# Second product of the FFN: part 7 after all chunks of parts 5, 6 and 3, on the bank of parts 1 and 6, with part 4 on that; the last norm regrouped; the first loads in small pieces

## The chip, the core and the metric

The kernel runs as one program on one core of a Trainium2 chip. The core has a matrix engine (TensorE; PE in the profile, PEld for its weight loads), three elementwise engines (VectorE or DVE, ScalarE or ACT, GpSimd or POOL), a synchronising engine (SyncE, SP), and 16 DMA engines. The metric is the device time of one execution in microseconds, the median of several runs. Before the change it was 1905.4 us (three runs, 1904.87 to 1906.9).

## What is computed

Two layers of a bidirectional encoder over 512 tokens of width 1024, everything in float32:

```python
for l in range(L):
    x = x + 0.5 * swiglu(rms_norm(x, ffn1_norm[l]), ffn1_w_in[l], ffn1_w_out[l])
    x = x + mixer(rms_norm(x, mix_norm[l]), mix_w_in[l], ...)
    x = x + 0.5 * swiglu(rms_norm(x, ffn2_norm[l]), ffn2_w_in[l], ffn2_w_out[l])
return rms_norm(x, final_norm)

def swiglu(x, w_in, w_out):
    g, u = jnp.split(x @ w_in, 2, axis=-1)
    return (jax.nn.silu(g) * u) @ w_out
```

So there are four feed-forward blocks (FFN), each with a first product (1024 to 2 x 2816) and a second (2816 to 1024). The change touches the second product of all four, the very beginning of the kernel, and the final norm.

## The kernel before

**Precision.** Each float32 operand is split into a high part (rounded to what TensorE reads as `fp32r`) and a low part (the rest). A product is three matmuls: high by high, low by high, high by low. For a weight tile the high part is made on ACT (line 181, or 176 with the sign changed) into `whi`, the low part on DVE (line 184 or 177) into `wlo`; there are three buffers of each. For an activation tile `split` and `hl` do the same (lines 298 and 299, or 301 and 302 with a gain).

**Weights.** A *granule* is 128 x 1024 numbers, 512 KB: two contraction tiles of 512 columns. `stage_items` lists all granules in the order of use. `Stream` issues their loads on SP's queue up to eight ahead into nine `raw` buffers; a second granule may be added to one by an accumulating DMA on POOL's queue (line 152) or by DVE (line 166).

**Strassen form.** The big products are done as seven block products, numbered 1 to 7, out of two-by-two blocks. In the second product of an FFN the contraction is cut in two halves, and each half into three chunks c = 0, 1, 2 of 3, 4 and 4 tiles (`CHUNK`), so each of the seven parts is done as three chunk products. One chunk product adds into a *pair* of PSUM banks, one for each block of 128 tokens. `steps` (line 667) is the order of chunk products: part 1 for all chunks, part 2 for all chunks, then 5, 6, 7, 3 for one chunk after the other, then part 4 for all chunks. `make(i)` prepares the activation operand of step i (a difference or sum on DVE in `comb`, line 659, then the split), and is called up to two steps ahead. For parts 1, 2 and 4 a granule is loaded as it is. Parts 5 and 7 load `d` and then add `c`, or `c` and then `a`, with the accumulating DMA; part 6 adds `a` to what part 5 left, and part 3 then adds `b`, both on DVE.

**Which bank holds what.** Parts 1 and 6 share one pair (`o1`): after part 1 has been subtracted from one quadrant of x, part 6 goes on adding into the same banks. Parts 7 and 4 share another pair (`o7`). Parts 2, 5 and 3 have one each. `update(ps, i, j, sign)` (line 662) adds or subtracts a pair to a quadrant of the residual x, on DVE, two instructions (line 665), one for each bank. In one FFN there are ten such updates, so 20 instructions.

**Order inside a chunk product.** `product` (line 458) takes granule by granule; `late_low` (line 449) issues, for a set of (bank, tile) pairs, the high and low activation matmuls with the high weights (lines 453, 454), and then those with the low weights (line 456). By default a granule serves both token blocks before the next granule comes. With `by_block` all granules serve token block 0 first and then block 1; before the change only the very last chunk product of the kernel uses it.

**Next stage.** `nxt.squares` sums the squares of a finished quadrant of x on ACT (line 335). `nxt.quad` transposes a finished quadrant for the next stage: eight PE transposes, then ACT and DVE work. In the three FFNs that are not the last one, quadrants (1,1) and (0,1) are transposed within part 4, chunk 0, inside a block where the order on DVE and ACT is the program's own.

**The start.** The gains (128 x 48) are loaded on ACT's queue (line 1506), and transposed x tiles and weight granules alternately on SP's (lines 1512 and 150): the first two x tiles (256 KB) on their own, then two by two; the first weight granule in two pieces. Nine matmuls on a tile of zeros (`warm`, line 138) run before anything has landed; ACT writes one column of `warm` by a Tanh (line 135), which also loads the table of that function. The first block is a plain product (`plain`, line 564): for each of eight contraction tiles, twelve matmuls into four banks named `cl`. `Norm.given` (line 342) scales an x tile by its gain, splits it, and keeps the scaled numbers in `raw` tiles named `xr` (line 350).

**The end.** In the last FFN, after part 4, x is normalised and written out. `gained` multiplies a half row block of x by the final gain on DVE (line 921); `scaled` multiplies a row block by its inverse root on ACT (line 926) and starts its transfer from SP's queue (line 927); `whole` does both at once on DVE (line 933). Row blocks 2 and 3 are finished early; for 0 and 1 the last quadrant of x comes from part 4, and `inverse` (line 391) works out one inverse root from the two sums of squares: a square root on ACT, then four small DVE instructions (lines 398 to 402). All of this is in an order written out by hand, and queued behind the last `wlo` of the kernel.

Of the kernel before, what the change touches and what calls it, by code (L numbers as in the profile page):

```python
# [29 lines left out]
WARM = 9  # L30
AHEAD = 2
# [61 lines left out]
def encoder_kernel(  # L93
    ctx: ExitStack, tc: tile.TileContext, xin, xtr, wst, gains, gfin, gbias, rpb, dft, chan, mask, ident_in, rot, out
# [40 lines left out]
    S.activation(warm[:, 0:1], ones, AF.Tanh)  # L135
# [5 lines left out]
    class Raw:  # L141
# [3 lines left out]
        def load(self, parts=1):  # L145
            if self.t is None:
                self.t = raw_pool[0](self.n)
                for c in range(0, self.n, self.n // parts):
                    cs = slice(c, c + self.n // parts)
                    nc.sync.dma_start(out=self.t[:, cs], in_=wst[GRAN_AT[self.key]][:, cs])  # L150
                if self.plus:
                    G.dma_start(out=self.t, in_=wst[GRAN_AT[self.plus]][:, 0 : self.n], accum_op=ALU.add)  # L152

    class Item:
        def __init__(self, raw, add=None, neg=False, stage=0, parts=1, pieces=1, then=None):
            self.raw, self.add, self.neg, self.stage, self.parts = raw, add, neg, stage, parts
            self.pieces, self.then = pieces, then

        def load(self):
            self.raw.load(self.pieces)  # L160
# [8 lines left out]
        def prep(self, nxt):  # L169
            n = self.raw.n  # L170
            hi = wp.tile([P, 1024], F32R, tag="whi", name=nm("whi"), bufs=3)[:, 0:n]
            lo = wp.tile([P, 1024], F32R, tag="wlo", name=nm("wlo"), bufs=3)[:, 0:n]
            t = self.raw.t
# [4 lines left out]
            else:  # L178
                for c in range(0, n, n // self.parts):
                    cs = slice(c, c + n // self.parts)  # L180
                    S.activation(hi[:, cs], t[:, cs], AF.Copy)  # L181
                    if nxt:
                        nxt.summed()
                    self.last = V.tensor_tensor(lo[:, cs], t[:, cs], hi[:, cs].bitcast(F32), ALU.subtract)  # L184
            if self.then:
                G.dma_start(out=t, in_=wst[GRAN_AT[self.then]][:, 0:n], accum_op=ALU.add)
            self.out = (hi, lo)

    def stage_items():
# [34 lines left out]
        def ffn(s):  # L224
            first = not items
            if first:
                for g in range(4):
                    add(Raw((s, "cl", g)), parts=2 if g < 2 else 1, pieces=2 if g == 0 else 1)
# [3 lines left out]
            for order in ((1,), (2,), (5, 6, 7, 3), (4,)):  # L232
# [85 lines left out]
    class Norm:  # L318
# [23 lines left out]
        def given(self, i, k, src):  # L342

            self.tiles(i)
            g = self.gain(4 * i + k)
            split(self.h[i][:, k, :], self.l[i][:, k, :], src, g)
# [37 lines left out]
        def terms(self, tb):  # L384

            e, f = small("e", 1), small("ef", 1)
# [1277 lines left out]
```

## Time and profile before

| what | value |
|---|---|
| median of three runs | 1905.4 us |
| the profiled execution's own time | 1904.67 us |
| its span, first to last instruction | 1902.9 us |
| PE busy | 1891.0 us (99% of the span), 9189 matmuls |
| DVE busy | 1606.4 us (84%) |
| ACT busy | 1161.2 us (61%) |
| transfers | 361.09 MB, on average 190 GB/s |
| granted TensorE clock, mean | 0.999 |

The span is the profile's; the execution's own time has 1.8 us more around it. The views read below are the profile page, the chain of work that ended last, the timeline (start, duration, engine, line, operation, tiles, and behind brackets the idle time before it with what ended it), the view of one tile's instructions (durations as least/median/most in ns), the table of stretches (busy time of each engine, then granted clock, DMA share and GB/s), and the DMA view. In the timeline a row such as `x2` stands for two instructions in a run; a PE duration includes the pipeline, so two matmuls follow each other more closely than their durations say.

### The profile page before, as it was taken

How to read it: one execution, taken by the hardware profiler on the slowest of the kernel's cores; microseconds unless marked ns; L12 is line 12 of the kernel's file. 1: busy time of each engine (PE TensorE's matmuls, PEld its weight loads, DVE VectorE, ACT ScalarE, POOL GpSimd, SP SyncE). 2: the span in 40 equal slices, each digit the busy share in tenths (PEclk: the TensorE clock that was granted, in tenths of full speed). 3: DMA queues.
4: the chain of work that ended last, by engine and by line, in shares of the span. 5: the costliest groups of instructions: out<-in, count | busy, mean ns of one | idle time of the engine just before them, and what ended most of it. 6: DMA issues, size and time to landing. Idle time of an engine off the chain costs nothing.

```text
span 1902.9 us, 25187 instructions
## 1 busy us (share of the span) xinstructions
PE 1891.0 (99%) x9189; PEld 1586.7 (83%) x9189; DVE 1606.4 (84%) x2000; ACT 1161.2 (61%) x1676; POOL 198.0 (10%) x246
## 2 busy tenths in 40 slices
PE   9999999999999999999999999999999999999998
PEld 7888888888888888888888888888888888888886
DVE  7877899586889987889997778995769899787899
ACT  6655665468566755566665556663675576555665
POOL 0101010310111010001010100103101101000010
PEclk9999999999999999999999999999999999999999
DMA  9777499322886776649877764974148867766594
GB/s 301 203 205 190 149 250 319 99 73 93 218 217 166 176 195 204 177 154 261 252 186 210 187 177 153 271 276 126 53 122 213 209 177 176 206 177 177 172 272 149
DMA packets 104924, 361.09 MB, mean 190 GB/s; under 512 B 12064, under 2 KB 14240, under 8 KB 104800
## 3 DMA queue, kind: packets, MB, share of 16 engines
q1 hardware_dynamic: 77856, 267.42, 40.1%
q0 software_dynamic: 26800, 92.04, 26.8%
q8 instruction: 72, 1.18, 0.2%
q14 instruction: 52, 0.43, 0.1%
q10 hardware_dynamic: 144, 0.02, 0.0%
HBM read 354.18 MB, written 2.11 MB: 187 GB/s over the span
## 4 chain that ended last, share of the span: by engine, by line
PE 99%; DVE 1%; ACT 0%; DVEq 0%; issue 0%; ACTq 0%
PE A L453 9%; PE A L454 9%; PE A L456 9%; PE o L453 7%; PE o L454 7%; PE o L456 7%; PE ps L292 5%; PE ps L293 5%; PE ps L294 5%; PE B L453 5%; PE B L454 5%; PE B L456 5%; PE C L454 2%; PE C L453 2%; PE C L456 2%; PE tr L546 2%
## 5 line engine op out<-in xcount | busy, mean ns | idle before, releaser
L181 ACT ACTIVATE whi<-raw 128x1024 fp32r<-128x1024 f32 (+1 forms) x528 | 546.4, 1037 | 418.9 <-PE A L454 124.6
L184 DVE TENSOR_TENSOR wlo<-raw,whi 128x1024 fp32r<-128x1024 f32 (+1 forms) x528 | 627.8, 1194 | 186.5 <-ACT whi L181 183.7
L152 POOL DMA_DIRECT2D raw<-in_wst_dram x158 | 136.2, 872 | 1282.0 <-DMA raw<-in_wst_dram 678.3
L166 DVE TENSOR_TENSOR raw<-raw,raw 128x1024 f32<-128x1024 f32 (+1 forms) x146 | 172.2, 1189 | 1.2
L454 PE MATMUL A<-whi,xl 128*128 128x512 f32 x384 | 149.5, 389 | 0.0
L453 PE MATMUL A<-whi,xh 128*128 128x512 f32 x384 | 149.4, 389 | 0.0
L456 PE MATMUL A<-wlo,xh 128*128 128x512 f32 x384 | 110.5, 389 | 0.0
L176 ACT ACTIVATE whi<-raw 128x1024 fp32r<-128x1024 f32 (+1 forms) x79 | 81.6, 1035 | 39.0 <-PE A L454 10.2
L177 DVE SCALAR_TENSOR_TENSOR wlo<-raw,whi 128x1024 fp32r<-128x1024 f32 (+1 forms) x79 | 92.9, 1190 | 11.6 <-ACT whi L176 11.6
L639 ACT ACTIVATE th<-sn,rh 128x512 f32<-128x512 f32 x80 | 56.9, 715 | 69.8 <-DVE sn L528 69.8
L523 ACT ACTIVATE sn<-A 128x512 f32<-128x512 f32 x96 | 56.4, 589 | 51.3 <-PE A L456 51.2
L456 PEld LDWEIGHTS A<-wlo,xh 128*128 128x128 f32 x384 | 72.1, 188 | 15.0
L454 PEld LDWEIGHTS A<-whi,xl 128*128 128x128 f32 x384 | 72.1, 188 | 14.8
L453 PEld LDWEIGHTS A<-whi,xh 128*128 128x128 f32 x384 | 72.1, 188 | 14.8
L453 PE MATMUL B<-whi,t1h 128*128 128x512 f32 x192 | 76.2, 397 | 0.0
L453 PE MATMUL A<-whi,t3h 128*128 128x512 f32 x192 | 75.3, 392 | 0.0
L453 PE MATMUL C<-whi,xh 128*128 128x512 f32 x192 | 74.9, 390 | 0.0
L453 PE MATMUL A<-whi,t2h 128*128 128x512 f32 x192 | 74.9, 390 | 0.0
L454 PE MATMUL B<-whi,t1l 128*128 128x512 f32 x192 | 74.8, 390 | 0.0
L454 PE MATMUL A<-whi,t3l 128*128 128x512 f32 x192 | 74.8, 390 | 0.0
L454 PE MATMUL C<-whi,xl 128*128 128x512 f32 x192 | 74.7, 389 | 0.0
L454 PE MATMUL A<-whi,t2l 128*128 128x512 f32 x192 | 74.7, 389 | 0.0
(410 smaller groups left out, 4785.7 us busy)
## 6 DMA issues: line engine op xcount, KB each, us to landing
raw<-in_wst_dram SPq DMA_DIRECT2D x466, 512.0 KB
raw<-in_wst_dram POOLq DMA_DIRECT2D x162, 512.0 KB, 7.7
raw<-in_wst_dram SPq DMA_DIRECT2D x30, 256.0 KB
vs<-v SPq DMA_DIRECT2D x12, 256.0 KB
bw<-in_rpb_dram SPq DMA_DIRECT2D x32, 68.0 KB
x<-in_xin_dram SPq DMA_DIRECT2D x4, 512.0 KB
raw<-in_wst_dram POOLq DMA_DIRECT2D x8, 256.0 KB, 8.1
dft<-in_dft_dram POOLq DMA_DIRECT2D x8, 256.0 KB, 6.0
```

The costliest lines, as they stand in the source:

```text
L152: G.dma_start(out=self.t, in_=wst[GRAN_AT[self.plus]][:, 0 : self.n], accum_op=ALU.add)
L166: V.tensor_tensor(self.raw.t, self.raw.t, self.add.t, ALU.add)
L176: S.activation(hi, t, AF.Copy, scale=-1.0)
L177: self.last = V.scalar_tensor_tensor(lo, t, -1.0, hi.bitcast(F32), ALU.mult, ALU.subtract)
L181: S.activation(hi[:, cs], t[:, cs], AF.Copy)
L184: self.last = V.tensor_tensor(lo[:, cs], t[:, cs], hi[:, cs].bitcast(F32), ALU.subtract)
L292: PE.matmul(ps, lh, rh, start=start, stop=False, skip_group_check=again)
L293: PE.matmul(ps, lh, rl, start=False, stop=False, skip_group_check=again)
L294: PE.matmul(ps, ll, rh, start=False, stop=stop, skip_group_check=again)
L453: PE.matmul(ps, lh, rh, start=start, stop=False, skip_group_check=again)
L454: PE.matmul(ps, ll, rh, start=False, stop=False, skip_group_check=again)
L456: PE.matmul(ps, lh, rl, start=False, stop=stop, skip_group_check=again)
```

## The change

It has three parts.

**1. The second product of each FFN.** The order of chunk products becomes: part 1, part 2, then 5, 6, 3 for one chunk after the other, then part 7 for all chunks, then part 4 for all chunks; the granules are listed in the same order. Part 7 now adds on into the pair of parts 1 and 6, and part 4 adds on into the same pair, so `o7` is gone; a quadrant that took two updates (one from each pair) takes one. The last chunk of part 7 and the first of part 4 are issued by token block. The transposes of quadrant (1,1) move from chunk 0 of part 4 to chunk 1.

**2. The end.** Row block 3 is finished before the last updates, one small term of row blocks 0 and 1 is made for both at once, row block 0 goes out in two halves, and row block 1 is multiplied by the final gain first; then ACT scales one half and sends it from ACT's own queue while DVE scales the other half, sent from SP's queue.

**3. The start.** The Tanh writes another tile than `warm`. The gains lie ahead of the transposed x in one array and come with the first x tile in one transfer; POOL copies them to their place. The first four x tiles and the first two granules come in pieces of 256 KB, x tile and weight piece in turn. The splits of the first four tiles are written out by hand, in a fixed order on DVE and ACT; the high part of the first two weight pieces is made on DVE instead of ACT. For the first two tiles the matmuls are ordered as all high by high, then all low by high, then all high by low.

```diff
-            for order in ((1,), (2,), (5, 6, 7, 3), (4,)):
+            for order in ((1,), (2,), (5, 6, 3), (7,), (4,)):
...
+            steps.append((3, c, lambda c=c: part(1, 1, c)))
+        for c in range(3):
             steps.append((7, c, lambda c=c: comb(part(0, 1, c), part(0, 1, c), part(1, 1, c), ALU.subtract)))
-            steps.append((3, c, lambda c=c: part(1, 1, c)))
...
-            key = {6: 1, 4: 7}.get(m, m)
+            key = {6: 1, 7: 1, 4: 1}.get(m, m)
...
-                ps[key], made.pop(i), list(range(len(CHUNK[0][c]))), c == 0 and m in (1, 2, 3, 5, 7), c == 2,
-                m in (4, 6), by_block=late and i == len(steps) - 1,
+                ps[key], made.pop(i), list(range(len(CHUNK[0][c]))), c == 0 and m in (1, 2, 3, 5), c == 2,
+                m in (4, 6, 7), by_block=(m, c) in ((7, 2), (4, 0)) or late and i == len(steps) - 1,
...
                     make(i + 2)
-                    nxt.quad(1, 1)
                     nxt.quad(0, 1)
             make(i + 2)
+            if m == 4 and c == 1 and not late:
+                nxt.quad(1, 1)
...
-            if m == 4 and c == 1:
-                update(ps[1], 1, 0, 1)
...
             elif m == 6:
-                update(ps[1], 1, 1, 1)
-            elif m == 7:
-                update(ps[7], 1, 1, 1)
-                nxt.squares(1, 1)
                 update(ps[1], 0, 1, -1)
...
+            elif m == 7:
+                update(ps[1], 1, 1, 1)
+                nxt.squares(1, 1)
...
+                    update(ps[1], 1, 0, 1, (0,))
+                    nxt.squares(1, 0, (0,))
+                    root = [nxt.inverse(b, e[:, b : b + 1], f[:, b : b + 1]) for b in range(2)]
+                    next(root[0])
+                    gained(0, 0)
+                    gained(0, 1)
+                    next(root[0])
+                    next(root[0])
+                    scaled(nxt, 0, 0)
+                    update(ps[1], 1, 0, 1, (1,))
+                    nxt.squares(1, 0, (1,))
+                    next(root[1])
+                    gained(1, 0)
+                    gained(1, 1)
+                    scaled(nxt, 0, 1)
+                    next(root[1])
+                    next(root[1])
+                    o_, _, _, to = half(1, 0)
+                    S.activation(o_, o_, AF.Copy, scale=nxt.inv[1])
+                    S.dma_start(out=to, in_=o_)
+                    o_, _, _, to = half(1, 1)
+                    V.tensor_scalar(o_, o_, nxt.inv[1], None, ALU.mult)
+                    nc.sync.dma_start(out=to, in_=o_)
...
-    S.activation(warm[:, 0:1], ones, AF.Tanh)
+    S.activation(sp.tile([P, 8], F32, tag="sq", name="tanh", bufs=2)[:, 0:1], ones, AF.Tanh)
...
-    S.dma_start(out=gn, in_=gains)
...
+        for kt in range(4):
...
+            ws.items[kt // 2].raw.piece(kt % 2 * T, (kt % 2 + 1) * T)
+        ws.fetch(2)
+        G.tensor_copy(gn, first_gains)
...
+                S.activation(xh, src[kt], AF.Copy, scale=g)
+                if kt == 0:
+                    norm.given_raw(0, 0, src[0], g)
+                if kt < 2:
+                    V.tensor_copy(wh[:, z], t)
+                else:
+                    S.activation(wh[:, z], t, AF.Copy)
+                V.scalar_tensor_tensor(xl, src[kt], g, xh.bitcast(F32), ALU.mult, ALU.subtract)
+                V.tensor_tensor(wl[:, z], t, wh[:, z].bitcast(F32), ALU.subtract)
+                if kt:
+                    norm.given_raw(0, kt, src[kt], g)
```

131 lines of the change are left out of this document (74 added, 57 removed).

## The prediction

> **What bounds the kernel.** I read the page first, then the chain of waits, then the timeline at both ends and at the seams of the second product.
>
> ```profile
> span 1902.9 us, 25187 instructions
> ...
> PE 1891.0 (99%) x9189; PEld 1586.7 (83%) x9189; DVE 1606.4 (84%) x2000; ACT 1161.2 (61%) x1676; POOL 198.0 (10%) x246
> ...
> PE 99%; DVE 1%; ACT 0%; DVEq 0%; issue 0%; ACTq 0%
> ```
>
> PE sets the time: 99% of the span and of the chain. What is not PE is 1902.9 - 1891.0 = 11.9 us, and nearly all of it lies before the first matmul and after the last. The change leaves the number of matmuls as it is, so it can gain at the two ends alone, and lose wherever PE, which has no gap now, gets one.
>
> **The start now.** From the chain of waits and the timeline:
>
> ```profile
> 2.73 4.02 PE ps L138 x9
> 6.75 0.43 PE cl L453
> ...
> 7.61 0.35 PE cl L453
> ...
> 8.20 0.23 PE cl L453
> ```
>
> ```profile
> 0.90 0.27 DVE L134 MEMSET warm<- 128x256 uint32 x1
> 1.18 1.28 ACT L135 ACT_TABLE_LOAD   x1 [1.18 <-PEq L1653]
> ...
> 2.73 4.02 PE L138 MATMUL ps<-warm 128*128 128x512 bf16 x9 [2.73 <-ACT warm L135]
> ...
> 4.51 0.72 ACT L301 ACTIVATE xh<-xt,gn 128x512 fp32r<-128x512 f32 x1 [1.84 <-DMA gn<-in_gains_dram]
> 4.51 0.62 DVE L350 TENSOR_SCALAR xr<-xt,gn 128x256 f32<-128x256 f32 x2 [3.35 <-DMA gn<-in_gains_dram]
> ...
> 5.14 1.25 ACT L181 ACTIVATE whi<-raw 128x512 fp32r<-128x512 f32 x2
> ...
> 5.27 0.75 DVE L302 SCALAR_TENSOR_TENSOR xl<-xt,gn,xh 128x512 fp32r<-128x512 f32 x1
> ...
> 6.19 0.99 PE L453 MATMUL cl<-whi,xh 128*128 128x512 f32 x1
> ...
> 7.09 0.72 ACT L301 ACTIVATE xh<-xt,gn 128x512 fp32r<-128x512 f32 x1 [0.71 <-DMA xt<-in_xtr_dram]
> ...
> 9.87 0.39 PE L453 MATMUL cl<-whi,xh 128*128 128x512 f32 x1
> ...
> 12.59 0.39 PE L453 MATMUL cl<-whi,xh 128*128 128x512 f32 x1
> ```
>
> The nine warm-up matmuls wait for ACT's table load, not for data, and end at 6.75, when the first operands (xh at 5.23, the first half of whi at about 5.8) are long there. A matmul then still takes 0.43; the step is 0.23 from about 8. So contraction tile 0 ends only at 9.87; tile 1 takes 12.59 - 9.87 = 2.72, the full-speed price of twelve.
>
> **The start after.** `warm` is free at 0.90 + 0.27 = 1.17, so the warm-up ends by 1.2 + 4.02 = 5.2. The gains were the last to land (4.51); they now come with x tile 0, so I leave the first operation at 4.5. ACT makes xh to 5.2; DVE makes two xr to 5.1, then the new copy of 512 numbers. No row shows it; bounds are half of the 0.62 (one row of 256, so 0.31) and the 0.75 of L302. I take 0.62, half of L181's 1.25, the same work: whi is there at 5.75. Tile 0 then ends at
>
> - 5.8 + 2.72 = 8.5 if the clock is full by then: gain 1.35;
> - if the clock comes 5.0 us after the first warm-up (2.73 to about 7.75 now), at 6.2: one slow matmul, gain 1.15;
> - if it comes at 7.75 whatever PE did: 4.5 matmuls at 0.43, 7.5 at 0.227, end 9.45, gain 0.4.
>
> I take **-1.0**, nearest the second, with something for the copy. Bounds: -0.4, and -1.95 if x tile 0 lands well before the gains did and only the warm-up's end (5.2 + 2.72 = 7.9) counts. Tile 1's xh is due at 8.5 and would be there at 7.09 + 0.72 = 7.8; its second weight piece now follows x tile 1, the same bytes into the queue as x tile 1 is now, so 7.1 and 7.7 after the copy: 0.8 of cover, and each tenth beyond it costs a tenth. POOL's copy of the gains, not seen in the trace, has from 4.5 to that xh.
>
> The Trainium skill (TensorE: Matmul & The Clock Gate, Part 1) says that the clock is released after about 3.4 us of sustained work counted in free-running windows. Here the trace shows 5.0 us from the first warm-up. By that rule the moment can be anywhere from 4.6 to 8 after the change, which spans the three cases above.
>
> **The second product, on PE.** The count of matmuls is the same. But a part that goes on in a bank that DVE has read starts with a slow matmul:
>
> ```profile
> L453 PE MATMUL o<-whi,c6h x88: 389/389/477, 264.0 to 1867.0; 128*128 128x512 f32 x88
> ...
> L453 PE MATMUL o<-whi,c7h x88: 389/389/390, 268.2 to 1872.5; 128*128 128x512 f32 x88
> ...
> L453 PE MATMUL o<-whi,c4h x88: 389/389/475, 319.8 to 1892.9; 128*128 128x512 f32 x88
> ```
>
> Parts 6 and 4 have a longest one of 477 and 475 ns against 389; part 7, which opens a fresh bank, has none. After the change part 7 goes on too, and part 4 waits once for each bank: two more of 0.087 in each of four FFNs, 0.7. Bounds 0 and +0.7; I take **+0.5**.
>
> The new wait is the seam of parts 7 and 4. Part 4 may not touch a bank before `update` has read part 7's sum. The block order gives cover: bank 0 is complete while PE still does block 1 of part 7's last chunk, 12 matmuls or 2.72; for bank 1 there is block 0 of part 4's first chunk, three tiles, 9 matmuls or 2.04. How fast does DVE answer?
>
> ```profile
> 1867.95 0.39 PE L453 MATMUL o<-whi,c7h 128*128 128x512 f32 x1
> ...
> 1868.24 1.21 DVE L184 TENSOR_TENSOR wlo<-raw,whi 128x1024 fp32r<-128x1024 f32 x1
> 1869.38 1.28 DVE L665 SCALAR_TENSOR_TENSOR x<-o,x 128x512 f32<-128x512 f32 x2
> ...
> 1878.83 0.39 PE L453 MATMUL o<-whi,c4h 128*128 128x512 f32 x1
> ...
> 1879.24 1.28 DVE L665 SCALAR_TENSOR_TENSOR x<-o,x 128x512 f32<-128x512 f32 x2
> ```
>
> Part 6 ends as part 7 begins, at 1867.95; its update starts 1.43 later, behind a `wlo`. Part 3 ends at 1878.83, answered after 0.41. With 0.68 for one update a bank is free 1.1 to 2.1 after it is complete: inside 2.72, and 0.1 past 2.04 at worst. Four seams: 0 to +0.4; I take **+0.2**. Queued behind the update on DVE are only later `wlo` and activation splits.
>
> **DVE and the transfers.** In parts 5, 6, 7, 3 both are full:
>
> ```profile
> 1819.00:1835.30 16.30, 16.30 (x73) 13.51 (x72) 16.30 (x18) 11.86 (x16) 2.74 (x4) 1.00 0.99 298
> ...
> 1862.50:1868.00 5.50, 5.50 (x26) 4.55 (x25) 5.50 (x8) 2.03 (x2) 0.00 (x0) 1.00 0.46 149
> ...
> L665 DVE SCALAR_TENSOR_TENSOR x<-o,x x80: 669/678/691, 244.1 to 1894.0; 128x512 f32<-128x512 f32 x80
> ```
>
> DVE is busy 16.30 of 16.30, the DMA share is 0.99 and falls to 0.46 only near the end. The change takes four of the 20 updates of each FFN away (80 rows in all), 4 x 0.6 = 2.4 us of DVE, off the path. Against that, parts 5, 6, 3 without part 7 between them are DVE's heavy ones: with 1.14 for each full granule's step, chunk 1 has 4, 6 and 5 of them, 17.1 us in three products of 24 x 0.227 = 5.45, 16.3. That is 0.8 of debt a chunk, less for chunk 0; part 7 pays it back later (4.55 in 5.45). The updates taken away are worth more than the debt of 2.1, so I cost it at nothing; without that cover it would be 2.1 at most in each FFN. The accumulating transfers of part 7 now come together, but the same bytes are asked for and parts 5, 6, 3 alone ask for less than DMA gives now: nothing. The transposes of quadrant (1,1), a product later, are first needed by the next stage's second half: nothing.
>
> **The end.** PE's last matmul ends at 1893.34 + 0.61 = 1893.95.
>
> ```profile
> 1892.68 1.28 DVE L921 TENSOR_TENSOR o<-x,gf 128x512 f32<-128x512 f32 x2
> ...
> 1893.34 0.61 PE L456 MATMUL o<-wlo,c4h 128*128 128x512 f32 x2
> ...
> 1893.99 0.69 DVE L665 SCALAR_TENSOR_TENSOR x<-o,x 128x512 f32<-128x512 f32 x1
> 1894.00 1.15 ACT L926 ACTIVATE o<-o,r 128x1024 f32<-128x1024 f32 x1 [0.21 <-DVE o L921]
> ...
> 1895.06 0.61 ACT L335 ACTIVATE junk<-x 128x512 bf16<-128x512 f32 x1
> ...
> 1895.79 0.29 ACT L396 ACTIVATE sq<-ssq,e 128x1 f32<-128x1 f32 x1
> ...
> 1896.41 0.21 DVE L398 TENSOR_SCALAR mh<-ssq,ef 128x1 f32<-128x1 f32 x1
> ...
> 1897.03 0.21 DVE L402 TENSOR_SCALAR inv<-rt,inv 128x1 f32<-128x1 f32 x1
> 1897.28 1.41 DVE L933 SCALAR_TENSOR_TENSOR o<-x,inv,gf 128x512 f32<-128x512 f32 x2
> 1898.12 1.21 SPq L934 DMA_DIRECT2D out_dram<-o  x2
> ...
> GB/s 0 0 0 0 0 0 0 0 0 0 0 0 0 0 0 328 426 393 251 0 0 284 393 437 284 0 0 0 415 371 415 339 410 361 404 82 0 0 0 0
> ```
>
> Now: the last update ends at 1894.68, ACT's square waits for row block 3 (L926) until 1895.06, the inverse root is ready at 1897.24 because two gain products of row block 0 stand between, and two `whole` end at 1898.69. After: L926 is gone from there (a half, 0.72 as L301's 512, ends by then), the square starts at 1894.7, the root ends 0.73 + 0.29 later at 1895.75; DVE meanwhile multiplies row block 1 by the gain, 1894.68 + 1.28 = 1895.96; the inverse takes 1897.24 - 1896.41 = 0.83, to 1896.8; both halves then run at once on ACT and DVE (0.72, at most 0.75) to 1897.55. That is 1898.69 - 1897.55 = 1.15 earlier. The last stretch of transfers (eight slices of 0.375 us, from 1898.5 to 1901.4, 1.05 MB) runs at about 400 GB/s; after, a quarter of it (256 KB, 0.65) has left before: at best 1.8 earlier. I take **-1.3**; bounds -0.7 (only one `whole` saved) and -1.8. The gain products moved ahead of the last updates take the 1.28 of the update that leaves part 4, chunk 1.
>
> The Trainium skill (Trainium Kernel Development and Optimization, Key Constraints) says that transfers issued by several engines share the same 16 DMA engines, so ACT's queue saves issue time only. The rows here agree with it: about 400 GB/s is kept up from SP's queue alone.
>
> **The sum.** -1.0 + 0.5 + 0.2 - 1.3 = -1.6, from the profiled execution's 1904.67 to 1903.1. That execution lay 0.7 under the median of the runs, 1905.4; from there the forecast is **1903.8**. Its own range, from the bounds: -1.95 + 0 + 0 - 1.8 = -3.75 to -0.4 + 0.7 + 0.4 - 0.7 = 0, so 1901.65 to 1905.4.
>
> **Rivals.**
>
> *The seam stalls (slower).* Two splits instead of one stand ahead of each update: it starts 1.43 + 1.14 = 2.57 late and is done at 3.25. Bank 0 then holds PE 0.53, bank 1 1.21, together 1.74 and 7.0 in four FFNs: 1903.8 - 0.2 + 7.0 = 1910.6. It is slower than before by over 0.2% when the updates start more than about 2.4 late. For it: DVE has no free time there. Against it: every update in the rows starts within 1.43, and part 7 is DVE's light part.
>
> *Both ends at their best, no cost.* The first x tile lands before 4.2 and the table of the tail holds: -3.75, 1901.6. For it: the gains were the named releaser. Against it: the 256 KB that stand beside them were issued in the same moment.
>
> *The start gives nothing.* The clock comes at 7.75 all the same, or the 1 us is lost later because the weights come no sooner (DMA share near 1 from there): -0.4 + 0.5 + 0.2 - 1.3 = -1.0, 1904.4.
>
> **Chances.** Forecast 0.55, start without gain 0.2, both ends at best 0.14, seam 0.11. 0.2% (3.8 us) is about what a measurement of this kernel can tell from no change. Faster by more than that needs the second rival: 0.16 with what I have not seen. Slower: 0.12. Same: 0.72. The range, with the second rival and half of the first, is 1900.8 to 1907.0.
>
> **What would show it.** Warm-up from 1.2, tile 1 of `cl` starting near 8.8 instead of 9.87; c7h with a longest matmul near 475; no PE gap over 0.3 where c4h begins; four updates less in each FFN (L665's successor x64); from PE's last matmul to the span's end 7.6 instead of 8.95. Wrong if PE waits at the four seams, if DVE's debt reaches PE in parts 3 or 7, or if the first tiles wait for DVE.

## The result, and the profile after

| | before | after |
|---|---|---|
| median | 1905.6 us (6 runs, 1904.9 to 1906.9) | 1917.1 us (6 runs, 1911.3 to 1919.4) |
| ratio | | 1.0055, interval 1.0044 to 1.0066 |
| the profiled execution's own time | 1904.67 us | 1913.6 us |
| its span | 1902.9 us | 1911.5 us |

The change makes the kernel slower by 0.55%; the forecast was 1903.8. From the page of the changed kernel, its span and engines, and the chain of waits by engine:

```profile
span 1911.5 us, 25169 instructions
...
PE 1896.2 (99%) x9189; PEld 1585.9 (83%) x9189; DVE 1598.2 (84%) x1985; ACT 1161.0 (61%) x1676; POOL 198.4 (10%) x247
...
PE 92%; DVE 3%; DMA 3%; issue 2%; ACT 0%; POOL 0%; SPq 0%; DVEq 0%; POOLq 0%; ACTq 0%
```

Before, 99% of the chain was PE; now 8% of it leads through other engines and through transfers. The matmuls are the same 9189. Where the time went is read from the table of stretches, with the four stretches laid from the first matmul of part 1 to the last of part 4 in each FFN (length, then busy time of PE, PEld, DVE, ACT, POOL; granted clock, DMA share, GB/s). Before:

```profile
227.41:336.75 109.34, 109.34 (x504) 91.10 (x503) 108.83 (x121) 69.90 (x92) 10.85 (x13) 1.00 0.87 268
...
1787.30:1893.95 106.65, 106.65 (x479) 88.23 (x477) 105.72 (x122) 64.24 (x81) 10.39 (x12) 1.00 0.72 207
sum 434.67, PE 434.67 PEld 361.56 DVE 432.20 ACT 275.71 POOL 45.07; mean PE 108.67 PEld 90.39 DVE 108.05 ACT 68.93 POOL 11.27
```

After:

```profile
227.34:339.61 112.27, 109.99 (x504) 90.88 (x503) 108.53 (x124) 71.19 (x98) 10.91 (x13) 1.00 0.85 261
846.04:956.77 110.73, 110.01 (x504) 90.87 (x503) 108.30 (x111) 71.94 (x94) 12.87 (x15) 1.00 0.88 250
1175.24:1289.19 113.95, 111.54 (x504) 91.91 (x503) 108.62 (x124) 71.27 (x98) 10.94 (x13) 0.99 0.84 257
1795.58:1904.49 108.91, 107.82 (x479) 87.85 (x477) 105.09 (x122) 65.43 (x82) 10.39 (x12) 1.00 0.75 210
sum 445.86, PE 439.36 PEld 361.52 DVE 430.54 ACT 279.83 POOL 45.11; mean PE 109.84 PEld 90.38 DVE 107.63 ACT 69.96 POOL 11.28
```

Before, PE is busy in every moment of the second products (434.67 of 434.67). After, they take 445.86: 11.2 us more, which is more than the whole loss of that execution. The rest is a gain at the end: PE's last matmul ends at 1893.95 before and 1904.49 after, 10.5 later, and the span's end comes only 8.6 later. Outside the second products nothing else moved: the first of them starts at 227.34 against 227.41.

What PE waits for, from the view of waits (engine, line and tile that waits, what for: us in total, times, longest):

```profile
PE o L459 <- ACT c7h L303: 4.2, 2, 2.4
PE o L460 <- DVE c7l L304: 1.2, 2, 0.7
...
PE o L462 <- DVE wlo L190: 0.6, 1, 0.6
...
```

The dearest wait is for `c7h`, the high part of part 7's activations, in the first FFN and the third. Nothing names `x`, the update at the seam. Why `c7h` is late stands in the timeline of the first FFN, ACT and then PE:

```profile
310.38 1.06 ACT L187 ACTIVATE whi<-raw 128x1024 fp32r<-128x1024 f32 x1 [1.60 <-DMA raw<-in_wst_dram]
314.25 1.06 ACT L187 ACTIVATE whi<-raw 128x1024 fp32r<-128x1024 f32 x1 [2.81 <-DMA raw<-in_wst_dram]
315.21 1.04 ACT L303 ACTIVATE c7h<-at 128x1024 fp32r<-128x1024 f32 x1
...
313.91 0.61 PE L462 MATMUL o<-wlo,c7h 128*128 128x512 f32 x2
316.31 0.73 PE L459 MATMUL o<-whi,c7h 128*128 128x512 f32 x2 [1.78 <-ACT c7h L303]
```

Its input `at` was ready at 311.27. But `c7h` stands behind a `whi` in ACT's queue, and that `whi` waits 2.81 for a transfer: the last granule of part 7, which PE itself wanted only a granule later. The chain of waits names the transfer, and its like in the third FFN (1250.82, 11.86 long):

```profile
302.26 11.88 DMA raw<-in_wst_dram
```

These are accumulating transfers from POOL's queue. When POOL could issue them (bracket: its wait before):

```profile
287.10 1.75 POOL L155 DMA_DIRECT2D raw<-in_wst_dram  x2 [14.48 <-DVE wlo L190]
...
298.10 0.86 POOL L155 DMA_DIRECT2D raw<-in_wst_dram  x1 [6.44 <-DVE x L679]
300.98 0.86 POOL L155 DMA_DIRECT2D raw<-in_wst_dram  x1 [2.02 <-DVE x L679]
302.26 0.86 POOL L155 DMA_DIRECT2D raw<-in_wst_dram  x1 [0.42 <-issue]
```

The view puts the waits of 14.48, 6.44 and 2.02 before them down to work of DVE. An accumulating transfer adds to what a plain load has brought, and that load needs a free `raw` buffer. DVE frees one when it has made its `wlo`, or added it to another. What SP, which issues the plain loads, waits for from 255 to 320 us:

```profile
SPq L149 <- DVE raw L168: 35.3, 12, 5.3
SPq L149 <- DVE wlo L190: 12.6, 9, 4.6
```

That makes 47.9 us; the kernel before has 48.4 in the same stretch, so its loads, too, ran as DVE freed the buffers. DVE is busy without a break through parts 5, 6 and 3. What is new is that the DMA engines have time to spare, and then none. The second chunk before (as in all these rows, the last two numbers are DMA share, about 1 when full, and GB/s), and then the stretches after:

```profile
268.00:284.50 16.50, 16.50 (x75) 13.66 (x74) 16.43 (x16) 11.01 (x12) 2.56 (x3) 1.00 1.02 308
```

```profile
272.00:288.40 16.40, 16.40 (x74) 13.56 (x73) 16.40 (x15) 9.07 (x10) 1.92 (x3) 1.00 0.78 219
288.40:304.80 16.40, 16.40 (x74) 13.59 (x73) 16.40 (x19) 6.04 (x7) 3.89 (x5) 1.00 1.00 250
...
309.00:314.20 5.20, 5.20 (x25) 4.25 (x23) 3.49 (x3) 1.06 (x1) 0.00 (x0) 1.00 1.04 308
```

The DMA share is 0.78 in the second chunk of parts 5, 6, 3, where it was 1.02 with part 7 among them, and 1.00 to 1.05 from the third chunk on.

### The profile page after: what moved, and what is told of

Read it like the earlier page. It is cut to its first block, busy times and chain, and to the rows that moved or that the text cites. A ratio compares the mean times of both kernels' runs of the same rounds, so it can differ in the third digit from the quotient of the medians.

```text
span 1911.5 us, 25169 instructions
## 1 busy us (share of the span) xinstructions
PE 1896.2 (99%) x9189; PEld 1585.9 (83%) x9189; DVE 1598.2 (84%) x1985; ACT 1161.0 (61%) x1676; POOL 198.4 (10%) x247
## 3 DMA queue, kind: packets, MB, share of 16 engines
q1 hardware_dynamic: 78144, 267.18, 40.0%
q0 software_dynamic: 26800, 92.04, 26.8%
## 4 chain that ended last, share of the span: by engine, by line
PE 92%; DVE 3%; DMA 3%; issue 2%; ACT 0%; POOL 0%; SPq 0%; DVEq 0%; POOLq 0%; ACTq 0%
PE A L459 9%; PE A L460 9%; PE A L462 9%; PE ps L297 5%; PE o L460 5%; PE ps L298 5%; PE ps L299 5%; PE o L462 5%; PE o L459 5%; PE B L459 5%; PE B L460 5%; PE B L462 5%; DMA raw<-in_wst_dram 3%; PE C L460 2%; PE C L459 2%; PE C L462 2%
```

## The experiments

The theories were: A, part 7's accumulating transfers are late; B, DVE's debt out of parts 5, 6, 3 reaches PE; C, the seam of parts 7 and 4. Later D: A and B only together. "Second products" are the stretches of the tables above, in us, in the order of the FFNs (before: 109.3, 109.3, 109.3, 106.7).

### One part of the change at a time

Each kernel is the one before with the named hunks of the diff.

> The kernel before with the new order, banks and seams of the second product alone; its start and its end are those of before. Theory A (the new order is the whole of the loss: part 7's accumulating loads come together and land late): slower by 0.5 to 0.8%, about 1916 to 1920 us, with PE waiting before the first matmuls of o on c7h or a late wlo in every FFN, 1.3 to 4.3 us for each. Rival B (the new start leaves the weight stream behind, and the FFNs only show it): within 0.1% of before, 1904.5 to 1907 us.

> The kernel before with the new start alone. Theory A: 1904.5 to 1905.6 us; contraction tile 1 of cl starts about 1.6 us sooner than in the kernel before, and by matmul 180 nearly all of that is lost to waits on wlo (19 to 24 us) and on a late whi (39 us), so 0 to 1.0 us less. The prediction's own number: 1.0 us less. Rival B: 8 us or more slower, with waits in the second products.

> The kernel before with the regrouped last norm alone. Theory A: from PE's last matmul to the end of the span 7.0 us as in the changed kernel (8.95 in the kernel before), 2.0 us less in all, 1903.6 us. The prediction's own number: 1.3 us less, 1904.3. If the hand-written order ahead of the last updates holds PE in part 4: less than 1 us gained.

> The changed kernel with the second product as it was before (order, banks, seams). Theory A: the two gains add, 1902.5 to 1904 us, 0.1 to 0.15% less than before, and no PE gap over 0.5 us in the second products. Rival B: 8 us or more slower than before.

| kernel | median | ratio to before | second products |
|---|---|---|---|
| second product alone | 1916.9 | 1.0056 (1.0044 to 1.0069) | 113.4, 110.9, 114.2, 108.5 |
| start alone | 1905.6 | 1.0000 (0.9992 to 1.0009) | 109.3, 109.7, 109.3, 106.7 |
| end alone | 1905.3 | 0.9996 (0.9988 to 1.0005) | 109.3, 109.3, 109.3, 106.7 |
| start and end | 1905.0 | 0.9998 (0.9989 to 1.0007) | 109.3, 109.4, 109.3, 106.9 |

The new second product is the whole loss; rival B of these expectations, the start, is out. But start and end give nothing either, so both runs miss what was expected of them. Not even the 2 us that the end gives in the whole change are there: from PE's last matmul to the end of the span it takes 7.0 in the whole change, 9.4 with the end alone, 9.3 with start and end. The timeline of start and end shows why, DVE first and then ACT:

```profile
1889.30 1.27 DVE L679 SCALAR_TENSOR_TENSOR x<-o,x 128x512 f32<-128x512 f32 x2
1890.50 0.15 DVE L416 TENSOR_TENSOR ms<-ssq 128x2 f32<-128x2 f32 x1
...
1893.22 2.19 ACT L951 ACTIVATE o<-o,r 128x1024 f32<-128x1024 f32 x2 [1.66 <-DVE r L427]
1895.32 0.61 ACT L340 ACTIVATE junk<-x 128x512 bf16<-128x512 f32 x1
```

With the old second product two updates (1.27) still stand in part 4, and DVE begins with the norm 4.3 before PE's end at 1894.77. In the whole change it begins at 1897.75, 6.7 before the end. So ACT is still scaling row blocks 2 and 3 when the squares of block 0 could start. The end's gain belongs to the updates that the new second product leaves out.

### Which of the two is late: transfers, DVE, ACT's order, or the bunching

All four are the changed kernel with one edit. The first and the third leave out sums of weights that the result needs.

```diff
# no sum in part 7 (c in place of c + a)
-                        add(c)
+                        add(Raw(c.key, c.n) if order == (7,) else c)
# c7h first: last whi of part 7 behind the last c7h, on ACT
+                with tc.issue_after(high_of[0].ins) if self.behind else nullcontext():
+                    S.activation(hi, t, AF.Copy)
# thin sum in part 3
+                z = slice(0, 1 if self.thin else self.raw.n)
+                V.tensor_tensor(self.raw.t[:, z], self.raw.t[:, z], self.add.t[:, z], ALU.add)
# parts 2 and 7 in turn
-            for order in ((1,), (2,), (5, 6, 3), (7,), (4,)):
+            for order in ((1,), (5, 6, 3), (2, 7), (4,)):
```

> The changed kernel, but part 7 of the second products uses c alone in place of c + a: the accumulating transfers of part 7 are left out, and with them that sum. Everything else is as in the changed kernel. Theory A (part 7's accumulating transfers are too much for the DMA engines in the 15 us of PE that part 7 takes): the waits at c7h and c7l go (2.2 and 0.8 us in the first FFN, 2.8 and 0.6 in the third), 7 to 9 us less than the changed kernel, 1906 to 1910 us. Theory B (DVE's debt out of parts 5, 6 and 3 reaches PE): the waits stay, 1914 us or more. Theory C (the seam of parts 7 and 4): the same, 1914 or more.

> The changed kernel with one edge more: on ACT, the high part of the last granule of part 7 is issued after c7h of the last chunk, so that c7h does not stand behind a transfer. Theory A1 (what PE waits for is c7h behind that late granule in ACT's queue): the waits at c7h of 2.2 us in the first FFN and 2.8 in the third go or fall under 0.5, and no new one takes their place, 4 to 6 us less than the changed kernel, 1911 to 1913 us. Theory A2 (the granule itself is too late for PE): the wait moves to whi or wlo of that granule, the time stays within 2 us of the changed kernel's 1917. Theory B: no change.

> The changed kernel, but part 3's weight sum is made for one column of 1024 only (the rest of that sum is left out; the loads stay): 6 x 1.1 us less DVE work in each FFN, with the transfers as they were. Theory A: the wait at c3's wlo (0.9 us in the second FFN) and at c6 (0.6) go, those at c7h stay at 2 us or more in FFN 1 and 3; 1 to 4 us less than the changed kernel, 1913 to 1916 us. Theory B (DVE's debt is the cause): 8 us or more less, 1909 us or under, with no wait at c7h.

> The changed kernel with part 2's chunks moved behind parts 5, 6 and 3, in turn with part 7's (2, 7, 2, 7, 2, 7); the transposes of quadrants (0,1) and (0,0) change places. All transfers, sums, banks and the seam to part 4 are kept; only the accumulating transfers of part 7 have 30 us of PE instead of 15. Theory A: the waits at c7h go, each second product takes 109.3 to 110.5 us of PE (110.7 to 114 in the changed kernel), 1903 to 1907 us. Theory B: the debt of 5, 6, 3 stays, waits at c3 and c6 as before, 1912 us or more. Theory C (bank and seam): 1914 us or more.

| kernel | median | ratio to before | second products |
|---|---|---|---|
| changed | 1917.1 | 1.0055 | 112.3, 110.7, 114.0, 108.9 |
| no sum in part 7 | 1903.7 | 0.9991 (0.9981 to 1.0000) | 109.5, 110.7, 109.5, 106.8 |
| c7h first | 1911.2 | 1.0029 (1.0017 to 1.0041) | 111.9, 112.2, 111.0, 108.4 |
| thin sum in part 3 | 1903.4 | 0.9988 (0.9978 to 0.9997) | 109.4, 110.6, 109.4, 107.0 |
| 2 and 7 in turn | 1913.7 | 1.0042 (1.0027 to 1.0057) | 111.6, 112.1, 110.9, 109.9 |

Neither A nor B was right alone. Take the accumulating transfers away, and DVE's debt, all still there, costs PE nothing but 1.4 us in the second FFN, with waits at `c6l` and at a `wlo` of part 3. Take DVE's sums of part 3 away, and these two waits go, and the transfers, all still there, cost nothing. The 1.3 in the second FFN is then mostly another wait, for `x` at the seam. Together A and B cost 11.2.

Both edits changed more than they were meant to, though: they also moved `c7h` on ACT. In the first FFN its last chunk is at 315.2 in the changed kernel, behind the late `whi`. Without the sum it is at 311.4 and with the thin sum at 292.4, ahead of it. The next run puts the order alone at 6.0 us, so up to that much of the 13 us that each edit gives may be the order's. With the thin sum POOL issues the fourth accumulating transfer of part 7 at 293.43, where the changed kernel issues it at 298.10, but the last at 302.65, where that has 302.26; it lands at 311.86 in place of 314.15. So it fits the rows that DVE's debt acts by way of the buffers, but no run shows it apart from the order on ACT.

The other two moved the wait without removing it. Of PE's waits with `c7h` first, and then with parts 2 and 7 in turn:

```profile
PE o L462 <- DVE x L682: 2.2, 3, 1.1
PE o L463 <- DVE c7l L307: 2.0, 3, 1.3
```

```profile
PE o L459 <- DVE x L679: 3.3, 6, 1.1
```

`c7h` is gone from both, so its place in ACT's queue was what PE waited for (A1), and the order on ACT alone is worth 6.0 us. But behind it stand `c7l`, which DVE makes after the `wlo` of the granule before, whose transfer is late too (it lands at 311.14), and `x`, the update at the seam of parts 7 and 4, up to 1.1 us late. In the changed kernel the stall at `c7h` had covered the seam. Parts 2 and 7 in turn was a miss for theory A as first put: part 7 had twice the time, but the second products still took 9.7 us more than before. Its last accumulating transfer was issued no sooner (302.34).

### More room for the transfers

```diff
-        ... tile([P, 1024], F32, tag="raw", name=nm("raw"), bufs=9)[:, 0:n]
+        ... tile([P, 1024], F32, tag="raw", name=nm("raw"), bufs=10)[:, 0:n]
-FETCH = 8
+FETCH = 9
```

> The changed kernel with ten raw buffers in place of nine, and loads issued nine granules ahead in place of eight (room from one junk tile in place of two). Nothing is left out. Theory D (neither cause is enough by itself: DVE, late out of part 3, holds the raw buffers, so part 7's loads start late, and their accumulating transfers, 9 to 12 us each, land late): one buffer more lets each load start a granule sooner, about 2.7 us; the waits at c7h fall under 0.5 us, and the time to 1906 to 1911 us. Theory A alone (the transfers are bound by their own rate, whenever they start): the waits stay over 1.5 us, 1914 to 1918. Theory B alone (DVE's work is late, whatever the transfers do): waits at c7l and c4l take their place, 1912 or more.

Median 1918.6, ratio 1.0071 (1.0057 to 1.0084): a miss in the total. But the second products take 109.4, 110.7, 109.5 and 106.7; the loss there is gone, as D has it. Part 7's last accumulating transfer is issued at 297.67 in place of 302.26 and lands at 310.37 in place of 314.15; `c7h`, at 311.8, now stands ahead of the last `whi` here too. What the total hides is a new loss in the mixers: from the end of the first second product to the start of the next 512.3 us, where the kernel before has 506.6.

Four runs went into that loss: the ninth granule in the FFNs alone; the new order and the ninth granule in the last FFN alone; this again with two junk tiles of one byte a number (the room for the tenth buffer had come from one junk tile in place of two); and the changed kernel with ten buffers, the ninth granule in the FFNs and two such tiles. The first three have the later sums of the next heading as well.

> The whole change with ten raw buffers, loads nine granules ahead inside the FFNs and eight in the mixers, and the two sums of xr behind the last wlo of the first block. Theory D with the mixers' loss of the run with ten buffers put down to the ninth granule there: second products at 109.4, 110.7, 109.5 and 106.7 us of PE (1.7 us over the kernel before in all), mixers as in the kernel before, start 1.2 us and end 2.0 us better: 1903.5 to 1905.5 us. If the mixers lose all the same: 1912 us or more.

> Old order, banks and seams of the second product in the first three FFNs, the new ones in the last alone, with ten raw buffers and nine granules ahead there; new start with the sums of xr behind the last wlo; new end. Theory: the first three second products take 109.3 us of PE, the last 106.7 to 107, from PE's last matmul to the end of the span 7.0 us (8.95 in the kernel before), matmul 180 at 46.6: 1902 to 1903 us, 2.5 to 3 us less than before. If the new end's gain hangs on more than the updates that the new order leaves out: 1904 us.

> The run with the new order in the last FFN alone, but with two junk tiles of one byte a number in place of one of two bytes (only the sum of the squares is used). If the mixers lost their 5 to 8 us each to the single junk tile: the waits at tr on x (2.7 us at 624 and 1577 us) go, the mixers take what they took before the change, and the time is 1902 to 1903.5 us, faster than both kernels by 2 us or more. If the tenth raw buffer itself costs the mixers: 1912 us or more.

> The changed kernel with ten raw buffers, nine granules ahead in the FFNs, and two junk tiles of one byte a number. Theory D (part 7's transfers start too late because DVE, late out of part 3, holds the raw buffers): the second products take 109.4, 110.7, 109.5 and 106.7 us as in the run with ten buffers, the mixers what they took before, and the whole is 1904 to 1906 us, 11 to 13 us less than the changed kernel. Rival (the mixers' loss belongs to the longer lead of the loads): 1910 us or more.

They took 1919.6, 1918.4, 1917.0 and 1920.5, so all four miss in the total. All keep the second products at 106.7 to 106.8 in the last FFN, and all lose in the mixers, with the same two waits, here with two junk tiles:

```profile
PE tr L377 <- DVE x L1503: 4.9, 2, 2.5
```

So neither the ninth granule in the mixers nor the single junk tile is to blame; the loss comes with a tenth buffer in that pool, which the mixers' later weights use too. How, the runs don't show.

### The start's lost gain, and a repair of the end on POOL

The start's sums are two DVE instructions, L618 and L619. In the changed kernel they stand ahead of the last `xl` and the last `wlo` of the first block (DVE, then PE):

```profile
16.84 1.22 DVE L618 TENSOR_TENSOR xr<-xr,xr 128x1024 f32<-128x1024 f32 x1
...
18.50 1.41 DVE L307 SCALAR_TENSOR_TENSOR xl<-xt,gn,xh 128x512 fp32r<-128x512 f32 x2
...
20.47 1.23 DVE L619 TENSOR_TENSOR xr<-xr,xr 128x1024 f32<-128x1024 f32 x1
21.61 1.22 DVE L190 TENSOR_TENSOR wlo<-raw,whi 128x1024 fp32r<-128x1024 f32 x1
...
22.89 0.73 PE L462 MATMUL cl<-wlo,xh 128*128 128x512 f32 x2 [0.40 <-DVE wlo L190]
```

```diff
+                with tc.issue_after(ws.items[ws.pos - 1].last.ins):
                     V.tensor_tensor(b11, b11, b12, ALU.subtract)
                     V.tensor_tensor(b12, b12, b22, ALU.subtract)
# and, in the first of the three runs only: row blocks 2 and 3 times gf on POOL
+                for tb in (2, 3):
+                    for q in range(2):
+                        gained(tb, q, G)
```

> The second product as before the change, with the new start and the new end, and two repairs. Start: the two sums of xr (L618, L619) are issued on DVE after the last wlo of the first block. End: the four gain products of row blocks 2 and 3 are made on POOL during part 4, off DVE. If the new start loses its lead to these sums on DVE: the waits of cl at 19 to 23 us (1.2 us in all) go, matmul 180 at 46.5 us or earlier (47.1 to 47.9 with the new start so far). If the new end gave nothing beside the old second product because DVE reaches the norm 2 us later: from PE's last matmul to the end of the span 7.0 to 7.5 us in place of 9.2. Together 1901.5 to 1903 us, faster than both kernels. If the lead at the start is lost to the weight stream in any case: 1903 to 1904.

> New start and new end with the old second product, and only the two sums of xr moved behind the last wlo of the first block. Theory (the new start loses its lead to these two sums on DVE): the waits of cl at 19 to 23 us go, matmul 180 at 46.6 us, 1903.5 to 1904.3 us, 1 us less than the same kernel without the move (1905.0). If the lead is lost to the weight stream in any case: 1905 us.

> The kernel before with the new start, and the two sums of xr behind the last wlo of the first block; old second product, old end. Theory (the two sums on DVE took the start's gain): matmul 180 at 46.5 us, where the kernel before and its variants with the old start have 47.2 to 48.0, the rest as before: 1904.0 to 1904.8 us. If the gain is lost again behind matmul 180: 1905.4.

Medians 1906.4 (with POOL, ratio 1.0009, 1.0000 to 1.0018), 1905.1 and 1904.5 (both 0.9999). In the total the first two miss what was expected, and no gain is clear of noise in the third. The start itself is as expected in the first two: the 181st matmul after the warm-up starts at 46.6 and 46.4 us, but at 47.2 in the third. Over all the traces here it starts at 46.4 to 47.2 in eight with this edit, at 47.1 to 47.9 in nine that have the new start without it, and at 48.0, 47.8 and 47.2 in three with the old start.

In the second and third run the gain is given back in the last FFN: 107.8 and 108.0 there in place of 106.7, with waits of 0.8 and 1.1 us at `c4l`. DVE's order there is that of start and end without the edit. The tile comes late because DVE waited 1.9 and 2.2 us in all for two `whi` some 40 us earlier, where start and end has one such wait of 1.1. The first of the two waits for an accumulating transfer. After that DVE has no free time to catch up. Whether the edit brings this about, the runs don't show. POOL's products were a repair that cost more than it gave:

```profile
1878.10 8.02 POOL L944 TENSOR_TENSOR o<-x,gf 128x512 f32<-128x512 f32 x4 [22.65 <-DVE x L680]
1882.64 2.32 DVE L190 TENSOR_TENSOR wlo<-raw,whi 128x1024 fp32r<-128x1024 f32 x1
...
1887.13 3.48 DVE L190 TENSOR_TENSOR wlo<-raw,whi 128x1024 fp32r<-128x1024 f32 x3
```

While POOL works, DVE takes 2.3 for what takes 1.16 a granule as soon as POOL is done; PE lost 3.8 in the last FFN, and the end gained 1.2 (8.1 from PE's last matmul to the end of the span, in place of 9.3).

### Room elsewhere

The general pool has two slots free in the FFNs. Part 7's chunk 1 goes there, and the mixers keep their nine buffers:

```diff
-                self.t = raw_pool[0](self.n)
+                self.t = (self.pool or raw_pool[0])(self.n)
+                        if order == (7,) and idx == 1:
+                            c.pool = lambda n: slot(F32, "raw", (1024,))[:, 0:n]
-                self.fetch(self.prepped + FETCH)
+                self.fetch(self.prepped + FETCH + (self.items[self.prepped].raw.key[1] in ('oa', 'ob', 'oc', 'od')))
```

> The whole change, with the later sums of xr and with part 7's chunk 1 in two free slots of the general pool in all four FFNs, nine granules ahead in the second products. Theory D: part 7's transfers start sooner, the second products take 109.4 to 109.6, 110.7, 109.4 to 109.6 and 106.8 us, mixers as before: 1904 to 1905.5 us, 12 us less than the changed kernel. Theory A alone (the transfers are bound by their rate whenever they start) or slots that are not free: waits at c7h over 1 us, 1912 us or more.

> Old second product in the first three FFNs, the new one in the last; new start with the later sums; new end. In place of a tenth raw buffer in the FFN's own pool, the two granules of part 7, chunk 1, are loaded into two free slots of the general pool, in the last FFN alone, with nine granules ahead in its second product. Theory D: mixers as before the change, last second product 106.7 to 107.2 us of PE, 7.0 us from PE's last matmul to the end: 1902 to 1903.3 us. If the slots are not free in time: waits at c7 in the last FFN, 1904 or more.

The whole change with this and the later sums: 1904.1, ratio 0.9993 (0.9984 to 1.0002), 13 us less than the change as it was. Its stretches:

```profile
226.07:335.56 109.49, 109.49 (x504) 90.94 (x503) 108.43 (x124) 71.30 (x98) 10.90 (x13) 1.00 0.88 268
841.93:952.68 110.75, 110.08 (x504) 90.86 (x503) 108.36 (x111) 71.92 (x94) 12.84 (x15) 1.00 0.88 251
...
sum 436.38, PE 435.70 PEld 360.86 DVE 430.08 ACT 280.12 POOL 45.04; mean PE 108.93 PEld 90.21 DVE 107.52 ACT 70.03 POOL 11.26
```

436.38 against 445.86, and PE is busy throughout but in the second FFN. Order, sums, banks, transfers and seam are those of the change; the room is new (with it the order on ACT changed as well: `c7h` at 310.71 now stands ahead of the last `whi`, and the start has the later sums). Against the run with `c7h` first, which has that order, it takes 7.0 less, of which the later sums can be about 1; the rest is the room's. POOL issues the last of them four us sooner:

```profile
294.81 0.86 POOL L155 DMA_DIRECT2D raw<-in_wst_dram  x1 [2.98 <-DVE x L682]
298.42 0.86 POOL L155 DMA_DIRECT2D raw<-in_wst_dram  x1 [2.75 <-DMA raw<-in_wst_dram]
```

The version with the new second product in the last FFN alone took 1902.7, ratio 0.9986 (0.9977 to 0.9995): the only one of all that computes the whole and whose interval lies under the kernel before. It has the old second product where the new one can only lose (109.3 three times), and the new one where the missing updates pay at the end (106.7; 7.0 from PE's last matmul to the end of the span).

## Why the prediction was wrong, point by point

**The step that failed** is "DVE and the transfers", costed at nothing; the four second products took 11.2 us more. Late transfers held a small tile on ACT, and PE waited for it.

*The transfers.* The prediction said of part 7's accumulating transfers: "the same bytes are asked for and parts 5, 6, 3 alone ask for less than DMA gives now: nothing". It averaged over all four parts, and it counted bytes. The page's DMA queues, after the change, show what it should have counted (megabytes, share of 16 engines; q1 are the plain loads, q0 the accumulating ones):

```profile
q1 hardware_dynamic: 78144, 267.18, 40.0%
q0 software_dynamic: 26800, 92.04, 26.8%
```

By these shares, of a span of 1911.5, a plain megabyte takes 0.400 x 1911.5 / 267.18 = 2.86 us of all 16 engines, an accumulating one 0.268 x 1911.5 / 92.04 = 5.57. A granule of 0.524 MB is 1.5 us plain and 2.9 accumulating, so one of part 7 is 4.4. An estimate from these rows: part 7 has 5.5 of them, 24 us of DMA in 66 x 0.227 = 15.0 us of PE. Parts 5, 6, 3 ask for 5.5 x (4.4 + 1.5 + 1.5) = 41 in 45. The sum, 65 in 60, is the same in any order, so 5 us had to be loaded ahead of PE before the change too. But now it is 9 for part 7 alone, and only the buffers carry a lead. These rows lay open before the change as well (267.42 MB at 40.1%, 92.04 at 26.8%).

*DVE's debt.* "The updates taken away are worth more than the debt of 2.1, so I cost it at nothing." The updates go where part 7 and part 4 are; the debt arises before. By itself it is small: 1.4 us in the second FFN, near nothing in the others, as the run without part 7's sums shows. But a late DVE frees `raw` buffers late, and the buffers were what the transfers lacked: nine raised to ten, or two slots elsewhere, took the loss away but for 1.4 us in the second FFN (with the order on ACT changed beside it). The prediction priced two queues one by one, found slack in each, and did not ask whether one uses up the other's. The bound of "2.1 at most in each FFN" did not hold for both together, 2.8 on the mean and 4.6 in the third.

**The start**, -1.0: alone it gave -0.2 by the median, -1.5 to +1.7 by the interval. Its first rows came out better than forecast:

```profile
1.23 4.02 PE L139 MATMUL ps<-warm 128*128 128x512 bf16 x9 [1.23 <-DVE warm L135]
...
3.68 0.72 ACT L1549 ACTIVATE xh<-xt 128x512 fp32r<-128x512 f32 x1 [1.45 <-DMA xt<-in_xtr_dram]
...
8.19 1.17 PE L583 MATMUL cl<-whi,xh 128*128 128x512 f32 x4
```

The warm-up is at 1.2 as said, the first operation at 3.68 in place of 4.5, tile 1 at 8.19 in place of 8.8. The rival "the start gives nothing, or it is lost later" is what happened, by another mechanism than the one named: two sums on DVE ahead of the last weights, not the weight stream.

**The slow first matmuls**, +0.5 in four FFNs: with room for the transfers the first and third FFN are 0.15 and 0.06 over the kernel before, the last 0.09, one or two matmuls of 0.087. But the reason was wrong. Part 7 goes on in a bank that DVE has read, and none of its matmuls with `c7h`, with which it begins, is slow (longest 393 ns in that run). The long matmuls stand right behind the transposes `tr`, whatever the bank. The view of the tile, and then the timeline of part 4:

```profile
L461 PE MATMUL o<-whi,c7h x88: 389/389/393, 303.6 to 1877.7; 128*128 128x512 f32 x88
```

```profile
322.95 0.81 PE L379 MATMUL tr<-ident,x 128*128 128x128 f32 x6
323.52 0.48 PE L461 MATMUL o<-whi,c4h 128*128 128x512 f32 x1
```

So it is in the kernel before: the long matmuls at 263.97 (`c6h`) and 325.59 (`c4h`), read in the prediction as the price of the bank, come behind transposes too, and in the last FFN, where none stand there, parts 6 and 4 have no such matmul. The first FFN's second product has three groups of transposes before and five after, because those of quadrants (1,1) and (0,1) no longer stand in one group.

**The seam**, +0.2, and its rival: no wait for `x` in the changed kernel. That was cover by the worse stall; with `c7h` first the seam cost 2.2 in three places. So updates can come late enough to hold PE, as the rival had it.

**The end**, -1.3: 8.95 became 7.03, so -1.9, beyond the bound of -1.8; the term was under-sized. From PE's last matmul to the last scaled half it takes 3.4 (4.7 before), where the prediction had 3.6. The transfers behind that take 3.6 in place of 4.2, nearly all of the 0.65 that it allowed at best. The sentence that the gain products "take the 1.28 of the update that leaves part 4" was right, and it is the reason that the end gives nothing alone.

The median of the changed kernel lies 3.5 us above its profiled execution; that part the trace doesn't place. Of the four longer executions three have a lower mean clock (0.995 to 0.997, against 0.998), which would fit more stretches of halved clock like the one shown at the end; that isn't shown.

## What to carry to other kernels

Before regrouping work, lay each queue's demand over the time of the new groups, not over their sum: DMA time by kind of transfer (here an accumulating transfer took twice a plain one), and ask how many buffers carry the lead. When two queues are near full, price them together: the one that frees the buffers sets when the other may start. A stall in the profile also hides the next one; a fix of the order on one engine may only show what stood behind it.

## What the runs showed of the hardware

- By the page's shares, an accumulating transfer took 5.57 us of the 16 engines for a megabyte, a plain one 2.86.
- The first matmul behind a group of PE transposes took 0.48 in place of 0.39, whatever bank it went to.
- With POOL at an elementwise product, DVE's two-input instructions took 2.32 in place of 1.21. The Trainium skill (SBUF — State Buffer, Who interferes with whom) says that a DVE instruction with two SBUF inputs contends with a GpSimd instruction that reads SBUF; the rows agree.
- The clock. By the durations of the first matmuls, it came 5.0, 3.2 and 2.8 us after the first warm-up matmul in three traces with the same start (the kernel before, second product alone, end alone). In the changed kernel it was halved for 3.41 us after PE had waited 2.4 us in the third FFN, which costs half of that, 1.7 us, and is the 0.75 (last columns: clock, DMA share, GB/s) in this stretch of the changed kernel:

```profile
1262.00:1268.00 6.00, 3.59 (x10) 2.24 (x10) 4.13 (x4) 3.79 (x4) 0.56 (x1) 0.75 1.03 417
```

The Trainium skill (TensorE: Matmul & The Clock Gate, Part 1) puts the loss of the full clock at an idle window of about 3.4 us. Here shorter gaps were enough, 2.4 us in this trace and 1.9 with the second product alone (316.3). But not always: in the changed kernel 1.8 us passed at the full clock (316.3), with ten buffers 2.5 and 2.4 (625.5 and 1578.6). So a stall of about 2 us can be dearer than it looks.
